# A two-layer encoder at 512 tokens: the feed-forward norm's factor goes into the operand from the third up block on

## Chip, cores and metric

The kernel runs on one core of one Trainium2 chip. The metric is device time in microseconds (us) of one execution. Three runs of the kernel before took 1310.16, 1311.35 and 1311.37 us; the median is 1311.35 us. Engines are named as in the profile: PE is TensorE (matmuls), PEld its weight loads, DVE is VectorE, ACT is ScalarE, POOL is GpSimd, SP the engine that issues the DMAs.

## The reference

Two layers, each an attention mixer, a cross-attention over 256 memory tokens and a feed-forward network with a depthwise convolution over positions; D_MODEL is 1024, D_FF is 2816, all in fp32. Only the feed-forward part matters here:

```python
def rms_norm(x, g):
    y = x32 * lax.rsqrt(jnp.mean(x32 * x32, axis=-1, keepdims=True) + EPS)
    return (y * g).astype(x.dtype)

def conv_ffn(h, w_up, conv_w, conv_b, w_down):      # h = rms_norm(x, norm_ffn[l])
    u = h @ w_up
    up = jnp.pad(u, ((0, 0), (1, 1), (0, 0)))
    u = up[:, :-2] * conv_w[0] + up[:, 1:-1] * conv_w[1] + up[:, 2:] * conv_w[2] + conv_b
    gate, val = jnp.split(u, 2, axis=-1)
    return (jax.nn.silu(gate) * val) @ w_down
```

The norm has a gain g per feature and a factor rsqrt(...) per token. The factor is the same for all features of a token, so it may be multiplied into h before the product with w_up or into u behind it.

## The kernel before

**Layout.** Activations lie transposed: 1024 features as 8 chunks of 128 partitions, 512 tokens along the free axis. `xT` holds the residual stream in fp32. Products are taken in fp32r with both operands split into a high and a low part; `mm3` issues three matmuls for each chunk: weight high times operand high, weight high times operand low, weight low times operand high.

**The norm's operand.** While the previous stage closes, `Norm.operand` writes for each chunk the high part of g times x (`ffn.hi`, on ACT) and its low part (`ffn.lo`, on DVE). These are two SBUF tiles of 8 x 512 columns with the tag `xg`, of which the pool has two buffers, so there is no room for a second pair. The token's factor isn't in them: it needs the sum over all chunks. `Norm.stat` and `Norm.spread` make it later as `ffn.rep`, 128 x 512, the factor of each token repeated on every partition.

**The up blocks.** The 22 blocks of 128 features of gate and value come in the order `UPS` (0, 2, 1, 3, ...). For each, `up_project` multiplies the 8 chunks with the block's two weight tiles (side 0 gate, side 1 value): 24 matmuls of 512 columns into one PSUM bank a side. Side 0 goes to the tag `sc`, side 1 to `tr`, with two banks each; the first block alone uses `mm`. `up_first` runs the first two blocks, and between them `ffn.stat()` and `ffn.spread()`. Then `up(UPS[n])` runs for n = 2 to 21, and from n = 5 on a `down_halved` step of the down projection stands behind each.

**Behind the product.** `up_finish` multiplies both PSUM sums by `ffn.rep` on DVE, in place. ACT then writes the centre tap and the bias into an SBUF tile, DVE adds the other taps from PSUM (two instructions of 504 columns and two of 7 for a side), ACT applies Silu, DVE multiplies gate and value, and `halved` splits the result and its sums of quarters into high and low for the down product (ACT copies, DVE subtractions).

**Weights.** Each weight tile comes by DMA into one of 3 `raw` buffers; ACT copies it to a high part, POOL subtracts to get the low part, 128 x 1024 each, into 4 buffers `hi` and 4 `lo`. A buffer comes free when PE has finished the block that read it.

**What sets the order.** No instruction is issued where it is written. `Taped` records every operation with its reads and writes; `Tape.plan` simulates the five engines with a table of costs and chooses an order for each engine; `Tape.play` (line 395 of before) issues it. So nearly all instructions carry line 395 in the profile, and a change in one place lets the planner reorder what stands behind it.

Of the kernel before, what the change touches and what calls it, by code (L numbers as in the profile page):

```python
# [14 lines left out]
ALU = mybir.AluOpType  # L15
# [11 lines left out]
KC = D // P  # L27
# [4 lines left out]
NF = D_FF // P  # L32
N_HALVED = [16, 16]
UPS = [j + (0, 1, -1, 0)[j % 4] if j < max(N_HALVED) else j for j in range(NF)]
N_COLS = 384
BEHIND = 5
EPS = 1e-6
BIG = 3.0e38
# [12 lines left out]
G_MIX, G_MQ, G_MKV, G_FFN, CW, CB = 0, 8, 16, 24, 32, 32 + 6 * NF  # L51
# [438 lines left out]
def encoder_kernel(ctx: ExitStack, tc: tile.TileContext, t: dict, out: list):  # L490
    nc = tc.nc
    tape = Tape()
    PE, ACT, DVE, POOL, SP = (
        Taped(tape, e, calls) for e, calls in zip(ENGINES, (nc.tensor, nc.scalar, nc.vector, nc.gpsimd, nc.sync)))
# [13 lines left out]
    def nm(s):  # L508
        uid[0] += 1
        return f"{s}_{uid[0]}"  # L510
# [10 lines left out]
    def rpair():  # L521

        hl = rtile((2, S))
        return hl[:, 0, :], hl[:, 1, :]

    def tmp(shape=(S,)):
        return tpool.tile([P, *shape], F32, tag="t", name=nm("t"))
# [10 lines left out]
    f = lambda ap: ap.bitcast(F32)  # L538
# [62 lines left out]
    def get_w(key, ahead=AHEAD):  # L601
        n = done[0]
        assert plan[n][0] == key, (plan[n][0], key)
        ahead = n + 1 + ahead
        while ahead < min(len(plan), n + 1 + AHEAD_HELD) and plan[ahead][4][1:] == "r":
            ahead += 1
        while len(ready) < min(len(plan), ahead):
            while len(raws) < min(len(plan), len(ready) + N_RAW):
                emit_raw()
            emit_split()  # L610
        while len(raws) < min(len(plan), len(ready) + N_RAW):
            emit_raw()
        done[0] += 1
        w = ready[n]
        ready[n] = None
        return w
# [32 lines left out]
    xT = [x[:, 0:S] for x in xg0]  # L649
    par = cpool.tile([P, DEPTH, NPAR], F32, name="par")  # L650
# [217 lines left out]
    for n in FIRST:  # L868
        if isinstance(n, (int, slice)):
            c, cs = (n, slice(0, S)) if isinstance(n, int) else (0, n)  # L870
            hi, lo, g = nn.hi[:, c, cs], nn.lo[:, c, cs], xg0[c][:, S : S + 1]
# [20 lines left out]
    for l in range(DEPTH):  # L892
# [599 lines left out]
        ffn = nn  # L1492
        acts = {}

        def up_project(j, side):
            pm = ps_t() if side else ps_s()
            gemm_T(pm, get_w(("up", j, side)), ffn.ops, range(KC), 0, KC - 1)
            return pm

        def up_first():  # L1500


            ws, us = [], []
            for side in range(2):
                ws.append(get_w(("up", 0, side)))
                us.append(ps_mm())
                gemm_T(us[side], ws[side], ffn.ops, range(KC - 1), 0, KC - 1)
            for side in range(2):
                gemm_T(us[side], ws[side], ffn.ops, [KC - 1], 0, KC - 1)
                if side == 0:  # L1510
                    ffn.stat()
            us1 = [up_project(UPS[1], 0)]
            ffn.spread()
            up_finish(0, us)
            us1.append(up_project(UPS[1], 1))
            up_finish(UPS[1], us1)

        def up(j):
            up_finish(j, [up_project(j, side) for side in range(2)])

        def up_finish(j, us):
            for side in range(2):
                DVE.tensor_mul(us[side], us[side], ffn.rep)
            cs = []
            for side in range(2):
                ch = side * NF + j
                u = us[side]
                w = [par[:, l, CW + i * 2 * NF + ch : CW + i * 2 * NF + ch + 1] for i in range(3)]
                cc = tmp()
                ACT.activation(cc, u, AF.Identity, bias=par[:, l, CB + ch : CB + ch + 1], scale=w[1])  # L1530
                for wi, dst, src in (
                    (w[0], slice(8, S), slice(0, S - 8)),
                    (w[0], slice(1, 8), slice(S - 8, S - 1)),
                    (w[2], slice(0, S - 8), slice(8, S)),
                    (w[2], slice(S - 8, S - 1), slice(1, 8)),
                ):
                    DVE.scalar_tensor_tensor(cc[:, dst], u[:, src], wi, cc[:, dst], op0=ALU.mult, op1=ALU.add)
                cs.append(cc)
            ACT.activation(cs[0], cs[0], AF.Silu)
            DVE.tensor_mul(cs[0], cs[0], cs[1])  # L1540
            if j < N_HALVED[l]:
                halved(j, cs[0])
                return
            acts[j] = rpair()
            ACT.copy(acts[j][0], cs[0])
            DVE.tensor_sub(acts[j][1], cs[0], f(acts[j][0]))
# [4 lines left out]
        def halved(j, u):  # L1551


            n = UPS.index(j)
            if n % 4 == 0:
                shared[:] = [rtile((2, 2, H))]
            if n % 2 == 0:
                waiting[n + 1] = u
                hl = shared[0][:, n // 2 % 2]
                ACT.copy(hl[:, 0], u[:, :H])  # L1560
                DVE.tensor_sub(hl[:, 1], u[:, :H], f(hl[:, 0]))
                return
            a, b = waiting.pop(n), u.rearrange("p (n q) -> p n q", n=2)
            hl, bh = shared[0][:, n // 2 % 2], rtile((2, 2, H))
            first, second = tmp((2, H)), tmp((2, H))
            hi, lo = rtile((4, H)), rtile((4, H))
            DVE.tensor_sub(first[:, 0], a[:, H:], a[:, :H])
            DVE.tensor_sub(second[:, 0], first[:, 0], b[:, 1])
            DVE.tensor_sub(first[:, 1], b[:, 1], a[:, H:])
            DVE.tensor_add(second[:, 1], b[:, 0], second[:, 0])  # L1570
            ACT.copy(bh[:, 0], b)
            DVE.tensor_sub(bh[:, 1], b, f(bh[:, 0]))
            for v, c in ((first, slice(0, 2)), (second, slice(2, 4))):
                ACT.copy(hi[:, c], v)
                DVE.tensor_sub(lo[:, c], v, f(hi[:, c]))
            q = {"11": (hl[:, 0], hl[:, 1]), "21": (bh[:, 0, 0], bh[:, 1, 0]), "22": (bh[:, 0, 1], bh[:, 1, 1])}
            for i, name in enumerate(("t1", "t3", "t2", "t4")):
                q[name] = hi[:, i], lo[:, i]
            quads[UPS[n - 1]] = q

        def down_halved(g, m):


            w = get_w(("down", g, m))

            def product(pm, a, b):
                for k in range(2):
                    mm3(pm, *w[a][k], *quads[4 * g + k][b], k == 0, k == 1)

            def pair(left, right):  # L1590
                pm = ps_mm()
                product(pm[:, :H], *left)
                product(pm[:, H:], *right)
                return pm

            left, right = (xT[m][:, c] for c in (slice(0, H), slice(H, S)))
            below = xT[m + 4].rearrange("p (n q) -> p n q", n=2)
            us = tmp((2, H))
            u, u2 = us[:, 0], us[:, 1]
            one = pair(("11", "11"), ("s2", "t2"))  # L1600
            ACT.copy(u, one[:, :H])
            DVE.tensor_add(left, left, one[:, :H])
            DVE.tensor_add(one[:, H:], one[:, H:], u)
            DVE.tensor_add(right, right, one[:, H:])
            ACT.copy(u2, one[:, H:])
            two = pair(("12", "21"), ("s4", "22"))
            DVE.tensor_add(xT[m], xT[m], two)
            three = pair(("22", "t4"), ("s1", "t1"))
            DVE.tensor_add(xT[m + 4], xT[m + 4], three)
            DVE.tensor_sub(right, right, three[:, H:])  # L1610
            four = ps_mm()[:, :H]
            product(four, "s3", "t3")
            DVE.tensor_add(four, four, u2)
            DVE.tensor_sub(below, below, four.unsqueeze(1).to_broadcast([P, 2, H]))
# [19 lines left out]
        def down_last(j0, nj):  # L1634
# [4 lines left out]
            SP.dma_start(gains, t["gfin"])  # L1639
            cs, tail = slice(0, N_COLS), slice(N_COLS, S)  # L1640
            ws = []
# [7 lines left out]
            for m in range(KC):  # L1649
                if m % 4 == 0:  # L1650
                    ws.extend(get_w(("down", n)) for n in range(len(ws), 3 + 3 * (m // 4)))
                rows.append(ps_mm()[:, :N_COLS])
                late = m < N_LATE
# [58 lines left out]
        for n in range(NF):  # L1712
            if n == 0:
                up_first()
            elif n > 1:
                up(UPS[n])
            if 0 <= n - BEHIND < N_HALVED[l]:
                down_halved(*divmod(n - BEHIND, 4))
# [159 lines left out]
```

## Time and profile before

| | |
|---|---|
| three runs, us | 1310.16, 1311.35, 1311.37 (median 1311.35) |
| the profiled execution, us | 1310.85 |
| its span, first to last instruction, us | 1308.8 |
| around the span, us | 2.05 |
| granted PE clock, share of full | 0.999 |
| DVE busy, us | 1058.4 (81%) |
| ACT busy, us | 739.2 (56%) |
| POOL busy, us | 808.9 (62%) |

The up blocks of layer 0 lie between about 300 and 600 us of the span, those of layer 1 between about 950 and 1270 us. In a row of the timeline the first number is the start in us, the second the time in which the row's instructions ran, then come engine, line, operation, output<-inputs (buffer numbers left out), shapes and count; in brackets stands how long the engine was idle ahead of it and what ended that. A PE row's time is that of the pipelined matmul up to its modelled end, so PE's pace is read from the starts.

### The profile page before, as it was taken

The numbers are of one execution on the slowest core, as the hardware profiler recorded it, in microseconds if no ns is written. First come the engines' busy times: TensorE is split into PE (matmuls) and PEld (weight loads), VectorE is DVE, ScalarE is ACT, GpSimd is POOL, SyncE is SP. The second block draws the span as 40 slices with busy tenths as digits, with TensorE's granted clock in tenths as the row PEclk, the third lists the DMA queues.
The fourth block names the chain that finished last, engine by engine and source line by source line (L and its number), as shares of the span: only waits on it lengthen the run. The fifth ranks groups of instructions, "written<-read, shape, count | busy, mean of one in ns | idle before, by whom it ended". The sixth has DMA issues, their size and how long they took to land.

```text
span 1308.8 us, 19578 instructions
## 1 busy us (share of the span) xinstructions
PE 1299.8 (99%) x6937; PEld 1121.7 (86%) x6937; DVE 1058.4 (81%) x2007; ACT 739.2 (56%) x1391; POOL 808.9 (62%) x607
## 2 busy tenths in 40 slices
PE   9999999999999999999999999999999999999997
PEld 8898888888888888888888988888888888888897
DVE  7679996766999998987555898956769999989865
ACT  7777686555545444544537767865645444444442
POOL 4465867627666677773726657774466667777651
PEclk9999999999999999999999999999999999999999
DMA  8752313313323333332355422232133333333321
GB/s 284 217 146 53 109 49 97 97 38 114 95 78 115 111 97 97 100 116 91 105 161 178 128 67 81 65 113 82 49 113 98 97 97 103 107 97 98 101 92 65
DMA packets 42609, 137.41 MB, mean 105 GB/s; under 512 B 5008, under 2 KB 8464, under 8 KB 42512
## 3 DMA queue, kind: packets, MB, share of 16 engines
q1 hardware_dynamic: 42080, 135.77, 34.4%
q8 instruction: 55, 0.90, 0.3%
q10 hardware_dynamic: 432, 0.39, 0.1%
q14 instruction: 42, 0.34, 0.1%
HBM read 126.18 MB, written 2.10 MB: 98 GB/s over the span
## 4 chain that ended last, share of the span: by engine, by line
PE 98%; DVE 1%; DMA 1%; ACT 0%; POOL 0%; issue 0%
PE mm L395 51%; PE sc L395 25%; PE tr L395 22%; DMA r<-r 1%; ACT t L395 0%; DVE t L395 0%; DVE s L395 0%; POOL t L395 0%; ACT r L395 0%; DVE sc L395 0%; DVE r L395 0%; ACT hi L395 0%; DVE xg L395 0%; ACT s L395 0%
## 5 line engine op out<-in xcount | busy, mean ns | idle before, releaser
L395 POOL TENSOR_TENSOR lo<-raw,hi 128x512 fp32r<-128x512 f32 (+2 forms) x236 | 438.3, 1870 | 305.0 <-ACT hi L395 304.4
L395 ACT CAST hi<-raw 128x512 fp32r<-128x512 f32 (+2 forms) x276 | 219.9, 817 | 185.7 <-PE sc L395 70.4
L395 PE MATMUL mm<-r,hi 128*128 128x512 f32 (+2 forms) x928 | 247.1, 346 | 0.0
L395 PE MATMUL sc<-xg,hi 128*128 128x512 f32 (+1 forms) x740 | 229.0, 391 | 0.0
L395 PE MATMUL tr<-xg,hi 128*128 128x512 f32 x672 | 207.1, 389 | 0.0
L395 PEld LDWEIGHTS mm<-r,hi 128*128 128x128 f32 x928 | 163.3, 189 | 21.6
L395 PE MATMUL mm<-r,lo 128*128 128x256 f32 (+2 forms) x496 | 165.6, 334 | 0.0
L395 PEld LDWEIGHTS sc<-xg,hi 128*128 128x128 f32 x740 | 137.1, 189 | 27.1 <-ACT hi L395 0.4
L395 PE MATMUL mm<-r,r 128*128 128x256 f32 (+2 forms) x1040 | 158.4, 293 | 0.0
L395 PEld LDWEIGHTS tr<-xg,hi 128*128 128x128 f32 x672 | 126.0, 188 | 26.1
L395 PEld LDWEIGHTS mm<-r,r 128*128 128x128 f32 x1040 | 142.4, 191 | 2.7
L395 POOL TENSOR_TENSOR r<-t,r 128x512 fp32r<-128x512 f32 x80 | 118.0, 1480 | 42.5 <-ACT r L395 42.2
L395 PE MATMUL sc<-xg,lo 128*128 128x512 f32 (+1 forms) x370 | 143.4, 389 | 0.0
L395 ACT CAST r<-t 128x512 fp32r<-128x512 f32 (+1 forms) x164 | 94.5, 588 | 86.4 <-DVE t L395 69.8
L395 PE MATMUL tr<-xg,lo 128*128 128x512 f32 x336 | 130.7, 389 | 0.0
L395 DVE TENSOR_TENSOR xT<-xT,mm 128x256 f32<-128x256 f32 (+2 forms) x216 | 116.6, 560 | 15.8 <-PE mm L395 9.5
L395 PE MATMUL mm<-xg,hi 128*128 128x512 f32 (+1 forms) x386 | 121.6, 394 | 0.0
L395 DVE TENSOR_TENSOR t<-t,t 128x512 f32<-128x512 f32 (+2 forms) x110 | 116.5, 1079 | 5.5 <-ACT t L395 2.9
L395 PE MATMUL mm<-hi,xg 128*128 128x512 f32 (+1 forms) x384 | 108.4, 358 | 0.0
L395 POOL TENSOR_SCALAR t<-t,s 128x512 f32<-128x512 f32 (+1 forms) x112 | 67.3, 616 | 65.2 <-DVE s L395 59.5
L395 PEld LDWEIGHTS mm<-r,lo 128*128 128x128 f32 x496 | 93.9, 189 | 9.5
L395 DVE TENSOR_TENSOR r<-t,r 128x512 fp32r<-128x512 f32 (+1 forms) x84 | 81.6, 992 | 8.3 <-ACT r L395 7.7
(138 smaller groups left out, 2422.9 us busy)
## 6 DMA issues: line engine op xcount, KB each, us to landing
raw<-in_w SPq DMA_DIRECT2D x207, 512.0 KB, 3.7
r<-r SPq DMA_DIRECT2D x30, 256.0 KB, 3.6
r<-in_bias SPq DMA_DIRECT2D x16, 384.0 KB, 4.6
raw<-in_w SPq DMA_DIRECT2D x8, 384.0 KB, 3.0
r<-in_memT SPq DMA_DIRECT2D x4, 512.0 KB, 7.1
xT<-in_w SPq DMA_DIRECT2D x7, 256.5 KB, 4.2
out<-xT SPq DMA_DIRECT2D x4, 384.0 KB, 3.4
r<-in_w SPq DMA_DIRECT2D x9, 128.0 KB, 4.1
```

Of the source, the lines that this page charges most:

```text
L395: call(*args, **kwargs)
```

## The change

From the third up block of each layer on (n = 2), the factor is in the operand. `scale_operands` is recorded once a layer, ahead of `up(UPS[2])`. For each of the 8 chunks it makes v = x * g * rep on DVE in a temporary (one instruction with two SBUF tensors), copies v to the high part on ACT and writes v minus the high part to the low part on POOL. High and low are the same tiles as before, overwritten in place: a chunk can be rewritten only when the second block's last matmul has read it. `up_finish` then leaves out its two multiplications by `ffn.rep` for the remaining 20 blocks. The first two blocks keep theirs.

```diff
-N_COLS = 384
+N_COLS, N_SCALED = 384, 2
...
+        scaled = []
+
+        def scale_operands():
+
+            scaled.append(True)
+            for c in range(KC):
+                v = tmp()
+                g = par[:, l, G_FFN + c : G_FFN + c + 1]
+                DVE.scalar_tensor_tensor(v, xT[c], g, ffn.rep, op0=ALU.mult, op1=ALU.mult)
+                hi, lo = ffn.ops[c]
+                ACT.copy(hi, v)
+                POOL.tensor_sub(lo, v, f(hi))
...
         def up_finish(j, us):
-            for side in range(2):
-                DVE.tensor_mul(us[side], us[side], ffn.rep)
+            if not scaled:
+                for side in range(2):
+                    DVE.tensor_mul(us[side], us[side], ffn.rep)
...
             elif n > 1:
+                if n == N_SCALED:
+                    scale_operands()
                 up(UPS[n])
```

How the planner then orders the engines is shown at the switch in layer 0; layer 1 has the same rows under other buffer numbers. Here `xg_637` is the operand's high part, `xg_638` its low part, `tr_772` the second block's side 1, and `xT_76` to `xT_79` are pairs of chunks of the residual.

On PE, before, from the end of the second block on; the third block's side 0 is `sc_783`, its side 1 (`tr_787`) follows when the 24 matmuls of side 0 are through:

```order
L395 MATMUL tr_772<-xg_638,hi_753 128x512
L395 MATMUL tr_772<-xg_637,lo_754 128x512
L395 MATMUL sc_783<-xg_637,hi_764 128x512
L395 MATMUL sc_783<-xg_638,hi_764 128x512
L395 MATMUL sc_783<-xg_637,lo_765 128x512
```

On PE, of the change, at the same place; the third block is now `sc_791` and `tr_795`:

```order
L395 MATMUL tr_772<-xg_638,hi_753 128x512
L395 MATMUL tr_772<-xg_637,lo_754 128x512
L395 MATMUL sc_791<-xg_637,hi_764 128x512
L395 MATMUL tr_795<-xg_637,hi_773 128x512
L395 MATMUL sc_791<-xg_638,hi_764 128x512
L395 MATMUL sc_791<-xg_637,lo_765 128x512
L395 MATMUL sc_791<-xg_637,hi_764 128x512
L395 MATMUL tr_795<-xg_638,hi_773 128x512
L395 MATMUL tr_795<-xg_637,lo_774 128x512
L395 MATMUL tr_795<-xg_637,hi_773 128x512
L395 MATMUL sc_791<-xg_638,hi_764 128x512
```

The two sides of the third block now run side by side: each chunk's six matmuls stand together, and the first that reads a chunk's low part is the third of its six. All other PE rows of the program are in the order of before; there are 5776 rows in both.

On DVE, of the change, behind the transposition that makes `rep_767`; before, the eight rows that write `t_783` to `t_790` weren't there, and `t_776`, the second block's side 0, went on at once:

```order
L395 TENSOR_TENSOR mm_756<-mm_756,rep_767 128x512
L395 SCALAR_TENSOR_TENSOR t_783<-xT_76,par,rep_767 128x512
L395 SCALAR_TENSOR_TENSOR t_784<-xT_76,par,rep_767 128x512
L395 SCALAR_TENSOR_TENSOR t_776<-sc_763,par,t_776 128x504
L395 SCALAR_TENSOR_TENSOR t_785<-xT_77,par,rep_767 128x512
L395 SCALAR_TENSOR_TENSOR t_786<-xT_77,par,rep_767 128x512
L395 SCALAR_TENSOR_TENSOR t_787<-xT_78,par,rep_767 128x512
L395 SCALAR_TENSOR_TENSOR t_788<-xT_78,par,rep_767 128x512
L395 SCALAR_TENSOR_TENSOR t_789<-xT_79,par,rep_767 128x512
L395 SCALAR_TENSOR_TENSOR t_790<-xT_79,par,rep_767 128x512
L395 SCALAR_TENSOR_TENSOR t_776<-sc_763,par,t_776 128x7
```

The taps of the first two blocks stand behind the eight products now, one row of them excepted. DVE has 1906 rows before and 1842 in the change: 80 multiplications less, 16 products more.

On POOL, of the change; before, the row on `lo_793` (then `lo_785`) was followed at once by the next weight's low part:

```order
L395 TENSOR_TENSOR lo_793<-raw_755,hi_792 128x1024
L395 TENSOR_TENSOR xg_638<-t_783,xg_637 128x512
L395 TENSOR_TENSOR xg_638<-t_784,xg_637 128x512
L395 TENSOR_TENSOR xg_638<-t_785,xg_637 128x512
L395 TENSOR_TENSOR xg_638<-t_786,xg_637 128x512
L395 TENSOR_TENSOR xg_638<-t_787,xg_637 128x512
L395 TENSOR_TENSOR xg_638<-t_788,xg_637 128x512
L395 TENSOR_TENSOR xg_638<-t_789,xg_637 128x512
L395 TENSOR_TENSOR xg_638<-t_790,xg_637 128x512
L395 TENSOR_TENSOR lo_797<-raw_766,hi_796 128x1024
```

All eight subtractions stand in one run, and `lo_797`, a weight of the fourth block, waits behind them. On ACT the copies of the first two chunks stand behind the first block's two centre taps, then the weight copy `hi_796`, whose buffer comes free with the last matmul of `tr_772`, then the copies of the other six chunks. SP's order of DMAs is unchanged.

## The prediction

> **What bounds the kernel now.** First the page: the span, the busy times, and the chain of work that ended last:
>
> ```profile
> span 1308.8 us, 19578 instructions
> ...
> PE 1299.8 (99%) x6937; PEld 1121.7 (86%) x6937; DVE 1058.4 (81%) x2007; ACT 739.2 (56%) x1391; POOL 808.9 (62%) x607
> ...
> PE 98%; DVE 1%; DMA 1%; ACT 0%; POOL 0%; issue 0%
> ```
>
> PE is busy for all but 9 us of the span and holds 98% of the chain. A busy PE may still run below its pace, so next I read its timeline where the third, fourth and fifth up block of layer 0 begin:
>
> ```profile
> 321.53 0.62 PE L395 MATMUL sc<-xg,hi 128*128 128x512 f32 x2
> 321.98 0.39 PE L395 MATMUL sc<-xg,lo 128*128 128x512 f32 x1
> 322.21 0.62 PE L395 MATMUL sc<-xg,hi 128*128 128x512 f32 x2
> ...
> 332.41 0.62 PE L395 MATMUL sc<-xg,hi 128*128 128x512 f32 x2
> ...
> 343.29 0.62 PE L395 MATMUL sc<-xg,hi 128*128 128x512 f32 x2
> ```
>
> Three matmuls take 322.21 - 321.53 = 0.68 us, 0.227 each. A block of 48 takes 332.41 - 321.53 = 10.88 us, which is 48 x 0.227, and so does the next. In these blocks PE waits for nothing, not for a tenth of a microsecond. Whatever DVE saves there, PE cannot give back; the change can only add a wait.
>
> **What is removed.** The multiplications by `rep`; the view of that tile's users counts them:
>
> ```profile
> L395 DVE TENSOR_TENSOR sc<-sc,rep x44: 683/689/700, 30.0 to 1260.9; 128x512 f32<-128x512 f32 x44
> L395 DVE TENSOR_TENSOR tr<-tr,rep x42: 686/690/700, 321.7 to 1266.3; 128x512 f32<-128x512 f32 x42
> ```
>
> 80 of these 86 go (2 sides, 20 blocks, 2 layers), at a median of 0.69 us: 55 of DVE's 1058 us. They lie beside matmuls that run without a gap, so for the path I take 0. The other end would be PE's 9 idle us of the whole span, but the blocks above hold none of them.
>
> **What is added, in the order of time.** Per layer: eight products on DVE, eight copies on ACT, eight subtractions on POOL, and on PE a wait for each chunk's low part. DVE of before around the switch in layer 0:
>
> ```profile
> 316.18 0.72 DVE L395 STREAM_TRANSPOSE rep<-tr 128x512 f32<-128x512 f32 x1 [5.70 <-PE tr L395]
> 316.93 0.70 DVE L395 TENSOR_TENSOR sc<-sc,rep 128x512 f32<-128x512 f32 x1
> 317.54 1.29 DVE L395 TENSOR_TENSOR mm<-mm,rep 128x512 f32<-128x512 f32 x2
> 318.73 1.77 DVE L395 SCALAR_TENSOR_TENSOR t<-sc,par,t 128x504 f32<-128x504 f32 x4
> ```
>
> POOL and ACT at the same time, and the row of `rep` in layer 1:
>
> ```profile
> 317.07 2.41 POOL L395 TENSOR_TENSOR lo<-raw,hi 128x1024 fp32r<-128x1024 f32 x1 [0.43 <-ACT hi L395]
> ```
>
> ```profile
> 315.94 1.05 ACT L395 CAST hi<-raw 128x1024 fp32r<-128x1024 f32 x1 [4.45 <-PE sc L395]
> 317.66 0.78 ACT L395 ACTIVATE t<-sc,par 128x512 f32<-128x512 f32 x1 [0.67 <-DVE sc L395]
> 318.34 1.44 ACT L395 ACTIVATE t<-mm,par 128x512 f32<-128x512 f32 x2
> 321.54 1.05 ACT L395 CAST hi<-raw 128x1024 fp32r<-128x1024 f32 x1 [1.76 <-issue]
> ...
> 329.13 0.61 ACT L395 CAST r<-t 128x512 fp32r<-128x512 f32 x1
> ```
>
> ```profile
> 962.19 0.72 DVE L395 STREAM_TRANSPOSE rep<-tr 128x512 f32<-128x512 f32 x1 [5.69 <-PE tr L395]
> ```
>
> The orders are the same until 318.73; there the first product is issued. PE wants the first low part at 321.98 (third matmul) and, with the two sides side by side, a further one every 6 x 0.227 = 1.36 us, the eighth at 331.50. So all hangs on how fast the low parts come. The old readers don't hold them up: the second block's side 1 begins 24 x 0.227 = 5.44 us ahead of 321.53 and lets go of a chunk every 0.68 us.
>
> A subtraction alone is short enough, but POOL and DVE hinder each other. DVE and POOL near the start of the program:
>
> ```profile
> 22.20 0.68 DVE L395 TENSOR_TENSOR lo<-raw,hi 128x512 fp32r<-128x512 f32 x1
> 22.80 1.77 DVE L395 TENSOR_TENSOR lo<-raw,hi 128x512 fp32r<-128x512 f32 x1
> ```
>
> ```profile
> 22.20 1.82 POOL L395 TENSOR_TENSOR lo<-raw,hi 128x512 fp32r<-128x512 f32 x1 [0.23 <-ACT hi L395]
> ...
> 22.20 3.53 POOL L395 TENSOR_TENSOR lo<-raw,hi 128x512 fp32r<-128x512 f32 x2 [0.23 <-ACT hi L395]
> 25.70 1.29 POOL L395 TENSOR_TENSOR t<-t,t 128x512 f32<-128x512 f32 x1
> ```
>
> POOL and DVE later, and DVE with POOL idle:
>
> ```profile
> 126.43 5.44 POOL L395 TENSOR_TENSOR lo<-raw,hi 128x512 fp32r<-128x512 f32 x4 [10.53 <-ACT hi L395]
> ```
>
> ```profile
> 126.89 2.57 DVE L395 SCALAR_TENSOR_TENSOR r<-r,par,r 128x256 fp32r<-128x256 f32 x2
> ```
>
> ```profile
> 11.30 1.41 DVE L395 SCALAR_TENSOR_TENSOR xg<-xT,xg 128x512 fp32r<-128x512 f32 x2
> ```
>
> Alone, POOL's operation takes 1.29 us (25.70). At 22.20 both engines begin one on two SBUF tensors: DVE ends at 22.88, POOL at 24.02, DVE's second at 24.57, POOL's second at 25.73. They go by turns, 1.16 for POOL and 0.55 for DVE, 1.71 a pair. The row at 126.89 has the products' own form, two SBUF tensors and a scalar: two of only 256 columns took 2.57 us beside POOL, where two of 512 took 1.41 with POOL idle (11.30). So I expect products and subtractions to take turns.
>
> [...]
>
> The walk: POOL holds the port until 317.07 + 2.41 = 319.48; the first product ends 0.55 later, at 320.03, the second at about 320.65. ACT has ended its centre taps by 319.78 and copies the first chunk by 320.70. Then DVE has one row on PSUM, and POOL runs the first subtraction alone, from 320.78 to 322.07. From there each of the six remaining products goes ahead of one subtraction: the seventh ends at 322.07 + 6 x 1.71 = 332.33. The copies (0.61 each) keep up, though the weight copy at 321.54 holds ACT until 322.59. With 0.08 for a handover (ACT's copy of 315.94 ends at 316.99, POOL starts at 317.07) PE begins on the seventh low part at 332.41 and 1.36 later, at 333.77, on the eighth, which it would have read at 331.50. **The wait is 2.27 us a layer.** In general it is 6 x (p - 1.36) + 0.17 for p us a pair. Bounds of p: 1.36, PE's own pace, if nothing hinders POOL (its 1.29 is then shorter), 0.17 us a layer; and 1.29 + 0.71 = 2.0 if both take their full time one behind the other, 4.0 us. I take the measured pair, 1.71.
>
> **What is late next.** The taps of the first two blocks stand behind the products, so PSUM banks come free later. The eighth product ends at 331.2. The rest of `sc_763` takes about 1.0 (of the 1.77 at 318.73), so its bank is free at 332.2; PE wants it at 332.41 + 2.27 = 334.7. ACT then has a copy, a table load, a Silu and a centre tap to run ahead of DVE's taps on `tr_772`:
>
> ```profile
> 323.29 1.28 ACT L395 ACT_TABLE_LOAD   x1
> 324.58 0.63 ACT L395 ACTIVATE t<-t 128x512 f32<-128x512 f32 x1
> ```
>
> 331.2 + 0.61 + 1.28 + 0.63 + 0.78 = 334.5; those taps end near 337.0, and PE wants the bank at 340.1. Going on like this I find the third block's side 0 free at about 344.2 (wanted at 345.6) and its side 1 at 349.7 (wanted at 351.0), with DVE meeting two of POOL's 2.4 us weight subtractions on the way. The margins are thin but positive: I count 0. At the other end two more such meetings, 4.8 us, against a margin of 1.4 would cost 3.4 us a layer; below 0 there is no room, as PE has no wait to lose. From then on each block spares DVE two multiplications, 1.4 us. The weight that now stands behind the subtractions, `lo_797`, ends near 333.6 + 2.4 = 336.0 and is wanted at 340.1.
>
> Layer 1 repeats layer 0 with 646.0 us added (962.19 against 316.18), so the sum is 2 x 2.27 = 4.5 us on the profiled execution's 1310.85: 1315.4 us. The median of the three runs lies 0.5 above that execution; beside it I forecast **1315.9 us**.
>
> **The rivals.** (1) **Not slower: the switch hides.** If the products got ahead of POOL, or POOL gave way less than at 22.20, interleaved PE, at 1.36 a chunk, would cover it: 2 x 0.17 = 0.3 us, 1311.7. It decides at p = 1.55, where the wait is 1.3 us a layer, 2.6 together: 0.2%, about what a measurement of this kernel can tell from no change. For it speaks only that POOL alone is faster than PE; against it, the rows with both engines at work. 16%. (2) **The backlog reaches PE**: banks come back late, 1.0 to 3.4 us a layer on top, 1317.9 to 1322.7. For it: the thin margins; against it: DVE's load falls with each block. 8%. (3) **The clock falls.** In this row of the windows PE idles for 0.77 of 10 us, and the granted clock is the column with 1.00:
>
> ```profile
> 0.00:10.00 10.00, 9.23 (x44) 8.18 (x45) 5.65 (x18) 7.08 (x17) 1.71 (x8) 1.00 0.71 218
> ```
>
> At the switch PE would idle for 2.3 of 13.1 us, in pieces of 0.35. If one such block ran at half clock its 10.88 us would double: up to 22 us for both layers, 1338. 4%. The Trainium skill, "TensorE: Matmul & The Clock Gate", section A second HAM failure mode, has micro-idles between groups of matmuls make the clock oscillate; the row doesn't bear it out, but its gaps are fewer. (4) **Faster by over 0.2%**: 2.6 of PE's 9 idle us would have to go, and its order outside the switch is unchanged. 2%.
>
> **How the numbers follow.** The forecast, 2.6 to 8 us slower, gets 70%; its own range is 1314.0 (p = 1.55) to 1319.4 (p = 2.0). The range is 1312.2 to 1320.5: it takes in a part of rival 1 below and a part of rival 2 above, and leaves out the rest. Faster 0.02; same 0.16 (rival 1); slower 0.82 (the forecast, rivals 2 and 3).
>
> **What would show it.** In the profile after: eight subtractions `xg<-t,xg` on POOL, near 1.7 us from one to the next; products `t<-xT,par,rep` on DVE stretched to about 1.7 us; the third block of either layer lasting 13.1 us instead of 10.88, the next ones 10.88 again, the clock at 1.00. I am wrong if the third block keeps 10.9 us (rival 1), if the blocks behind it are longer too (rival 2), or if the multiplications saved shorten anything on PE.

## The result, and the profile after

| | before | change |
|---|---|---|
| median of 8 runs each, us | 1311.09 (1309.96 to 1312.81) | 1315.46 (1314.29 to 1316.65) |
| ratio of times, 95% interval | | 1.0033 [1.0024, 1.0042] |
| span of the profiled execution, us | 1308.8 | 1312.9 |
| third up block, layer 0 / layer 1, us | 10.88 / 10.88 | 13.26 / 13.26 |
| DVE busy, us | 1058.4 | 1024.4 |

The change makes the kernel 4.4 us slower. First the page of the change:

```profile
span 1312.9 us, 19588 instructions
...
PE 1303.3 (99%) x6937; PEld 1120.2 (85%) x6937; DVE 1024.4 (78%) x1943; ACT 747.1 (57%) x1407; POOL 831.7 (63%) x623
...
PE 97%; POOL 1%; issue 0%; DMA 0%; ACT 0%; SPq 0%; DVE 0%
```

PE still reads 99% busy and has 3.5 us more of busy time, with as many matmuls as before. So the loss can't be found as idle time of PE. The starts of PE's rows show it. This is PE's timeline in the change, from the first matmul of the third block in layer 0 to the first of the fifth, with the same block of layer 1 behind it:

```profile
320.81 0.39 PE L395 MATMUL sc<-xg,hi 128*128 128x512 f32 x1
321.03 0.39 PE L395 MATMUL tr<-xg,hi 128*128 128x512 f32 x1
321.45 0.50 PE L395 MATMUL sc<-xg,hi 128*128 128x512 f32 x1
321.79 0.40 PE L395 MATMUL sc<-xg,lo 128*128 128x512 f32 x1
322.03 0.40 PE L395 MATMUL sc<-xg,hi 128*128 128x512 f32 x1
...
323.14 0.50 PE L395 MATMUL sc<-xg,hi 128*128 128x512 f32 x1
...
334.07 0.39 PE L395 MATMUL sc<-xg,hi 128*128 128x512 f32 x1
...
344.95 0.61 PE L395 MATMUL sc<-xg,hi 128*128 128x512 f32 x2
...
969.21 0.39 PE L395 MATMUL sc<-xg,hi 128*128 128x512 f32 x1
...
982.47 0.61 PE L395 MATMUL sc<-xg,hi 128*128 128x512 f32 x2
```

The third block takes 334.07 - 320.81 = 13.26 us, 2.38 more than before; the fourth takes 344.95 - 334.07 = 10.88 again; layer 1's third takes 13.26 too. Between the switches nothing changed: 969.21 - 334.07 = 635.14 us, against 967.54 - 332.41 = 635.13 in the kernel before. The third matmul of a chunk, the first that reads the low part, starts 0.42 us behind its forerunner (321.03 to 321.45) instead of 0.227, and the one behind it another 0.34 later. From chunk to chunk PE now needs 323.14 - 321.45 = 1.69 us, further on 1.71, not 1.36.

What it waits for is in the list of waits, on the row of the weight loads. The columns are engine, tile and line, then the releaser, the total in us, how often, and the longest:

```profile
PEld sc L395 <- POOL xg L395: 6.6, 14, 0.5
```

Fourteen times in the program (seven a layer) a weight load stands until POOL has written a low part. The wait is booked on PEld, while the matmul ahead is still counted as busy on PE. POOL and DVE at the switch in layer 0:

```profile
316.35 2.41 POOL L395 TENSOR_TENSOR lo<-raw,hi 128x1024 fp32r<-128x1024 f32 x1 [0.43 <-ACT hi L395]
320.09 12.77 POOL L395 TENSOR_TENSOR xg<-t,xg 128x512 fp32r<-128x512 f32 x8 [1.34 <-ACT xg L395]
```

```profile
315.46 0.72 DVE L395 STREAM_TRANSPOSE rep<-tr 128x512 f32<-128x512 f32 x1 [5.69 <-PE tr L395]
...
318.01 1.96 DVE L395 SCALAR_TENSOR_TENSOR t<-xT,par,rep 128x512 f32<-128x512 f32 x2
...
320.54 9.91 DVE L395 SCALAR_TENSOR_TENSOR t<-xT,par,rep 128x512 f32<-128x512 f32 x6
...
342.23 1.78 DVE L395 SCALAR_TENSOR_TENSOR t<-sc,par,t 128x504 f32<-128x504 f32 x4
```

Eight subtractions run without a break from 320.09 to 332.86; the first seven end 1.70 to 1.71 us apart. The seventh ends at 331.62, and PE's matmul that reads it starts at 331.67. Six products take 9.91 us beside them, 1.65 each. The users of `rep` over the whole program, with the least, median and greatest length in ns, say the same, and count what went:

```profile
L395 DVE SCALAR_TENSOR_TENSOR t<-xT,par,rep x16: 740/1776/1787, 318.0 to 977.1; 128x512 f32<-128x512 f32 x16
...
L395 DVE TENSOR_TENSOR sc<-sc,rep x4: 698/700/700, 30.3 to 964.6; 128x512 f32<-128x512 f32 x4
...
L395 DVE TENSOR_TENSOR tr<-tr,rep x2: 686/688/690, 331.4 to 979.8; 128x512 f32<-128x512 f32 x2
```

A product takes 0.74 us when nothing hinders it and 1.78 beside a subtraction. DVE lost 80 multiplications, 55 us, and its busy time fell by only 34, since the sixteen products are stretched by their turns with POOL and other rows moved as well. The windows of the third block show the clock, in the column behind the five engines' busy times:

```profile
320.80:334.10 13.30, 13.02 (x50) 8.49 (x49) 12.56 (x12) 7.28 (x11) 13.30 (x9) 1.00 0.06 23
```

The clock stays at 1.00; POOL is busy for the whole stretch. The span's +4.1 us is 2 x 2.38 = 4.76 for the switches, less 0.72 by which this execution was already ahead at the transposition that makes `rep` (315.46 against 316.18): a difference that arises before the change has any effect.

### The profile page after: what moved, and what is told of

It reads as the page before. It is cut to its first block, busy times and chain, and to the rows that moved or that the text cites. A ratio compares the mean times of both kernels' runs of the same rounds, so it can differ in the third digit from the quotient of the medians.

```text
span 1312.9 us, 19588 instructions
## 1 busy us (share of the span) xinstructions
PE 1303.3 (99%) x6937; PEld 1120.2 (85%) x6937; DVE 1024.4 (78%) x1943; ACT 747.1 (57%) x1407; POOL 831.7 (63%) x623
## 4 chain that ended last, share of the span: by engine, by line
PE 97%; POOL 1%; issue 0%; DMA 0%; ACT 0%; SPq 0%; DVE 0%
PE mm L395 52%; PE sc L395 24%; PE tr L395 21%; POOL xg L395 1%; DMA xT<-in_w 0%; SPq L395 0%; ACT xg L395 0%; DVE r L395 0%; ACT t L395 0%; POOL t L395 0%; ACT s L395 0%; ACT hi L395 0%; DVE s L395 0%
## 5 line engine op out<-in xcount | busy, mean ns | idle before, releaser
L395 POOL TENSOR_TENSOR lo<-raw,hi 128x512 fp32r<-128x512 f32 (+2 forms) x236 | 434.8, 1856 | 301.9 <-ACT hi L395 301.3
L395 ACT CAST hi<-raw 128x512 fp32r<-128x512 f32 (+2 forms) x276 | 220.1, 817 | 241.5 <-PE sc L395 90.1
L395 PE MATMUL mm<-r,hi 128*128 128x512 f32 (+2 forms) x928 | 247.1, 346 | 0.0
L395 PE MATMUL sc<-xg,hi 128*128 128x512 f32 (+1 forms) x740 | 232.9, 392 | 1.1 <-ACT xg L395 0.3
L395 PE MATMUL tr<-xg,hi 128*128 128x512 f32 x672 | 209.8, 389 | 0.0
L395 PEld LDWEIGHTS mm<-r,hi 128*128 128x128 f32 x928 | 163.2, 189 | 21.7
L395 PEld LDWEIGHTS sc<-xg,hi 128*128 128x128 f32 x740 | 136.8, 188 | 34.0 <-POOL xg L395 6.6
L395 PE MATMUL mm<-r,lo 128*128 128x256 f32 (+2 forms) x496 | 165.6, 334 | 0.0
L395 PE MATMUL mm<-r,r 128*128 128x256 f32 (+2 forms) x1040 | 158.4, 293 | 0.0
L395 PEld LDWEIGHTS tr<-xg,hi 128*128 128x128 f32 x672 | 126.0, 188 | 26.4
L395 PEld LDWEIGHTS mm<-r,r 128*128 128x128 f32 x1040 | 142.4, 191 | 2.7
L395 PE MATMUL sc<-xg,lo 128*128 128x512 f32 (+1 forms) x370 | 143.4, 388 | 0.0
L395 POOL TENSOR_TENSOR r<-t,r 128x512 fp32r<-128x512 f32 x80 | 116.3, 1458 | 35.6 <-ACT r L395 19.6
L395 DVE TENSOR_TENSOR xT<-xT,mm 128x512 f32<-128x512 f32 (+2 forms) x216 | 117.3, 560 | 19.6 <-PE mm L395 13.5
L395 PE MATMUL tr<-xg,lo 128*128 128x512 f32 x336 | 130.8, 389 | 0.0
L395 ACT CAST r<-t 128x512 fp32r<-128x512 f32 (+1 forms) x164 | 92.8, 587 | 54.9 <-DVE t L395 28.5
L395 PE MATMUL mm<-xg,hi 128*128 128x512 f32 (+1 forms) x386 | 121.5, 393 | 0.0
L395 DVE TENSOR_TENSOR r<-t,r 128x512 fp32r<-128x512 f32 (+1 forms) x84 | 99.0, 1202 | 27.1 <-ACT r L395 26.8
L395 PE MATMUL mm<-hi,xg 128*128 128x512 f32 (+1 forms) x384 | 108.4, 358 | 0.0
L395 DVE TENSOR_TENSOR t<-t,t 128x512 f32<-128x512 f32 (+2 forms) x110 | 101.5, 942 | 8.5 <-ACT t L395 4.9
L395 POOL TENSOR_SCALAR t<-t,s 128x512 f32<-128x512 f32 (+1 forms) x112 | 67.3, 617 | 63.4 <-DVE s L395 56.6
L395 PEld LDWEIGHTS mm<-r,lo 128*128 128x128 f32 x496 | 93.9, 189 | 9.5
```

What stands on the lines that cost most here:

```text
L395: call(*args, **kwargs)
```

## The experiments

The theory after the result: **DVE's products and POOL's subtractions take turns at SBUF**; a pair takes 1.71 us, and PE at 1.36 a chunk waits for the low parts. The rivals: the wait is made by something else in the chain (the copy on ACT, the new order of the sides on PE) and would stand without the turns; the multiplications removed bring a gain that the sum of 4.4 hides; a backlog on DVE has a part in it. Each edit below is made to the kernel with the change. With each edit the planner chooses its orders anew: only e8 keeps PE's order of the change row for row, and e3 has that of the kernel before. In e1, e2, e5 and e6 some matmuls of the next block stand among those of the block of the switch. A length below is therefore PE's time for 48 matmuls from the block's first one on, in layer 0 and in us; behind it stand the times beside the kernel before on the same chip:

| | third | fourth | fifth | time, us | before, us | ratio, 95% interval |
|---|---|---|---|---|---|---|
| before | 10.88 | 10.88 | 10.88 | | | |
| change | 13.26 | 10.88 | 10.88 | 1315.46 | 1311.09 | 1.0033 [1.0024, 1.0042] |
| e1: factor read from PSUM | 11.13 | 10.88 | 10.88 | 1310.66 | 1310.52 | 1.0002 [0.9993, 1.0011] |
| e2: switch two blocks later | 10.88 | 10.88 | 12.67 | 1319.07 | 1310.52 | 1.0065 [1.0053, 1.0078] |
| e3: removal alone | 10.88 | 10.88 | 10.88 | 1310.42 | 1310.52 | 1.0000 [0.9992, 1.0009] |
| e4: addition alone | 13.29 | 10.88 | 13.94 | 1321.39 | 1310.52 | 1.0083 [1.0069, 1.0097] |
| e5: every other product from PSUM | 12.34 | 11.35 | 10.88 | 1314.30 | 1310.34 | 1.0029 [1.0018, 1.0041] |
| e6: each product twice | 19.74 | 12.42 | 11.0 | 1332.57 | 1310.34 | 1.0169 [1.0155, 1.0182] |
| e7: subtraction on DVE | 12.61 | 13.11 | 11.0 | 1319.85 | 1310.34 | 1.0072 [1.0058, 1.0085] |
| e8: addition alone, planner blind to it | 13.26 | 13.52 | 11.71 | 1322.46 | 1310.34 | 1.0091 [1.0077, 1.0105] |

### e1: the products read the factor from PSUM

```diff
             scaled.append(True)
+            rep = ps_mm()
+            ACT.copy(rep, ffn.rep)
             for c in range(KC):
...
-                DVE.scalar_tensor_tensor(v, xT[c], g, ffn.rep, op0=ALU.mult, op1=ALU.mult)
+                DVE.scalar_tensor_tensor(v, rep, g, xT[c], op0=ALU.mult, op1=ALU.mult)
```

The products keep their number and their size; one of their two operands lies in PSUM, and the two change places in the instruction. The planner also moves taps between them.

> The factor is copied once a layer by ACT into a PSUM bank that is free then (tag mm), and the eight products read it from there, so each has one SBUF tensor and one PSUM tensor; number of products, copies, subtractions and PE's interleaving are those of the change. Theory (products and subtractions take turns because both engines work on two SBUF tensors): the subtractions follow each other in 1.25 to 1.3 us instead of 1.71, PE's third block lasts 10.9 to 11.3 us instead of 13.26, and the time is 1311.3 to 1312.0 us. Rival A (the chain product, copy, subtraction and its handovers is what is slow, wherever the operands lie): the block stays at 13 us and the time near 1315.5. Rival B (the late release of PSUM banks costs the time): one bank more is taken, so no gain, 1315.5 or more.

Measured: 1310.66 us, 0.14 above the kernel before, and a third block of 11.13 us. The group of the sixteen products (busy time, then ns of one, then idle time ahead), and POOL's timeline at the switch:

```profile
L395 DVE SCALAR_TENSOR_TENSOR t<-mm,par,xT 128x512 f32<-128x512 f32 x16 | 11.7, 741 | 0.0
```

```profile
321.47 2.55 POOL L395 TENSOR_TENSOR xg<-t,xg 128x512 fp32r<-128x512 f32 x2 [0.90 <-ACT xg L395]
324.30 5.07 POOL L395 TENSOR_TENSOR xg<-t,xg 128x512 fp32r<-128x512 f32 x4 [0.28 <-ACT xg L395]
329.32 2.41 POOL L395 TENSOR_TENSOR lo<-raw,hi 128x1024 fp32r<-128x1024 f32 x1
331.69 3.00 POOL L395 TENSOR_TENSOR xg<-t,xg 128x512 fp32r<-128x512 f32 x2
```

All sixteen products take 0.74 us, and four subtractions in a row 5.07, 1.27 each. So the turns go with the second SBUF operand, as the theory has it.

The time doesn't follow from that alone, since the planner gave this kernel another order as well. It put a weight subtraction ahead of the last two low parts, and the eighth comes at 334.69, 12.06 us behind the block's first matmul (322.63). In the change it comes 12.05 us behind (332.86 against 320.81), no later. PE doesn't wait for it here, because ten matmuls of the fourth block's side 0 stand ahead of the third block's last, which is the second of these rows:

```profile
335.57 0.39 PE L395 MATMUL tr<-xg,hi 128*128 128x512 f32 x1
335.80 0.39 PE L395 MATMUL tr<-xg,lo 128*128 128x512 f32 x1
```

In the change's order PE would want the eighth low part 331.50 - 321.53 = 9.97 us behind its first matmul, and would have waited some 2.1 us for this one. Without the weight subtraction, and with the products in time, two more steps of 1.27 behind the sixth low part (329.37) would bring the eighth 9.3 us behind, soon enough. Both are estimates from these rows: no run has the factor in PSUM together with the change's order. What e1 shows is the pace without turns, and that the copies on ACT and the rewriting in place, in this order, cost 0.25 us a layer at most. That turns at this pace make the wait is shown by the rows of the change, and by e5.

The version is only equal to the kernel before, a little better than expected: DVE is busy for 36.6 us less than there (1021.8), and PE, which sets the pace, has no work less.

### e3: the removal alone

```diff
             scaled.append(True)
-            for c in range(KC):
-                v = tmp()
...
-                POOL.tensor_sub(lo, v, f(hi))
```

> The multiplications behind the sums are left out from the third block on, and nothing is put in their place, so the factor is missing in 20 of 22 up blocks. Theory (PE is at its pace in the up blocks, so what DVE saves is worth nothing): DVE's busy time falls by 55 us, PE's blocks stay at 10.88 us and the time stays within 0.5 us of before, 1310.6 to 1311.6. Rival D (sparing DVE shortens something, and the change's 4.3 us are a larger cost less a gain): faster than before by 1 us or more, below 1310.

Measured: 1310.42 against 1310.52 us; every block 10.88. Its page:

```profile
PE 1299.0 (99%) x6937; PEld 1121.7 (86%) x6937; DVE 1005.4 (77%) x1927; ACT 736.4 (56%) x1391; POOL 805.1 (62%) x607
```

53 us of DVE are gone and the time has not moved. There is no gain hidden in the change's sum; its 4.4 us are all loss.

### e5: every other product from PSUM

```diff
+            rep = ps_mm()
+            ACT.copy(rep, ffn.rep)
...
-                DVE.scalar_tensor_tensor(v, xT[c], g, ffn.rep, op0=ALU.mult, op1=ALU.mult)
+                DVE.scalar_tensor_tensor(v, rep if c % 2 else ffn.rep, g, xT[c], op0=ALU.mult, op1=ALU.mult)
```

> As the run with the factor in PSUM, but only the products of chunks 1, 3, 5 and 7 read it there; those of 0, 2, 4 and 6 read the SBUF copy, as in the change. Theory (turns): half the turns are gone, so the mean pace of the subtractions is about 1.5 us and the third block lasts 11.2 to 12.2 us, between the 11.2 of all in PSUM and the 13.26 of none; the time is 1311.0 to 1313.5 us. Rival E (what helped was only that the planner ordered DVE otherwise once the rows were on PSUM): no value between the two is called for; the block is at one of the two ends.

Measured: 1314.30 us, above what was expected, with a third block of 12.34. Its subtractions end at 321.13, 322.84, 324.08, 325.78, 327.03 and 328.73: paces of 1.71, 1.24, 1.70, 1.25, 1.70, in step with where the product's operand lies. So the turns are taken product by product. The products from SBUF have their operands in e1's order too, so it isn't the swap that ended the turns there. The excess over the expectation is in POOL's rows behind them:

```profile
319.84 8.90 POOL L395 TENSOR_TENSOR xg<-t,xg 128x512 fp32r<-128x512 f32 x6 [1.33 <-ACT xg L395]
329.38 1.29 POOL L395 TENSOR_TENSOR xg<-t,xg 128x512 fp32r<-128x512 f32 x1 [0.65 <-ACT xg L395]
330.63 2.39 POOL L395 TENSOR_TENSOR lo<-raw,hi 128x1024 fp32r<-128x1024 f32 x1
332.99 1.74 POOL L395 TENSOR_TENSOR xg<-t,xg 128x512 fp32r<-128x512 f32 x1
```

The planner has put a weight subtraction of 2.39 us between the seventh and the eighth chunk; the eighth low part comes at 334.73. As in e1, matmuls of the fourth block fill a part of PE's time until then.

### e6: each product twice

```diff
                 DVE.scalar_tensor_tensor(v, xT[c], g, ffn.rep, op0=ALU.mult, op1=ALU.mult)
+                DVE.scalar_tensor_tensor(v, xT[c], g, ffn.rep, op0=ALU.mult, op1=ALU.mult)
```

> Each product is computed twice into the same tile, so DVE has two operations on two SBUF tensors for each subtraction of POOL; the output is that of the change. Theory (turns): a chunk takes 1.16 + 0.55 + 0.6, some 2.3 us, and the first low part comes a little later, so PE's third block lasts 16.5 to 18.0 us and the time is 1322 to 1326 us, more if the backlog reaches PE as well. Rival A (the chain product, copy, subtraction sets the pace, DVE's own load does not): the doubled product adds its 0.66 us once at the start only, the block lasts 13.5 to 14.5 us, 1316 to 1318.

Measured: 1332.57 us and a third block of 19.74, beyond every value expected. That it grew this far says that the products set the pace; that it grew by more than the theory's sum lies on POOL, as its rows and PE's show:

```profile
321.65 2.98 POOL L395 TENSOR_TENSOR xg<-t,xg 128x512 fp32r<-128x512 f32 x2 [2.66 <-ACT xg L395]
324.60 2.80 POOL L395 TENSOR_TENSOR lo<-raw,hi 128x1024 fp32r<-128x1024 f32 x1
```

```profile
328.65 0.79 PE L395 MATMUL sc<-xg,hi 128*128 128x512 f32 x1 [2.75 <-ACT xg L395]
...
330.61 0.63 PE L395 MATMUL sc<-xg,lo 128*128 128x512 f32 x1
331.04 0.63 PE L395 MATMUL sc<-xg,hi 128*128 128x512 f32 x1
331.46 0.63 PE L395 MATMUL tr<-xg,hi 128*128 128x512 f32 x1
```

A weight subtraction again stands between the chunks, holds DVE and so the next products, and PE idles for 2.75 us. From the first low part (322.93) to the eighth (341.06) 18.1 us pass; less the weight subtraction's 2.8 that is 2.2 us for each of the seven steps, near the theory's 2.3.

Behind the gap PE's matmuls start every 0.43 us instead of 0.227; the window of that stretch has the clock at half:

```profile
330.70:334.40 3.70, 3.70 (x10) 2.89 (x9) 3.70 (x5) 1.24 (x2) 1.76 (x2) 0.50 0.00 0
```

This slows PE but doesn't lengthen the block, since PE waits for operands again behind it:

```profile
338.48 0.50 PE L395 MATMUL sc<-xg,hi 128*128 128x512 f32 x1 [0.67 <-ACT xg L395]
```

Layer 1 bears it out: there the half clock lasts only from 986.7 to 990.0, in layer 0 from 327.9 to 334.6, and the block takes 19.73 us. As a measure of the pair's price e6 is rough, because of the weight subtraction.

### e7: the subtraction on DVE too

```diff
-                POOL.tensor_sub(lo, v, f(hi))
+                DVE.tensor_sub(lo, v, f(hi))
```

> The eight subtractions go to DVE, so DVE has product and subtraction of each chunk, 0.66 + 0.6 = 1.26 us when nobody disturbs it, and POOL only its weights. Theory (turns): each weight subtraction of POOL (2.4 us) that falls into the switch still stops DVE once, one or two of them; the third block lasts 11.5 to 13.5 us and the time is 1312 to 1316.5. Rival A (chain of three operations on engines that wait for each other): the chain is as long as before, 13.3 us or more, 1315.5 or more.

Measured: 1319.85 us, above the range, though the third block, 12.61, was within it. Here no subtraction of POOL's stands against the products, and DVE makes product and subtraction in 1.26 us together. But DVE meets POOL's weights, on DVE and POOL:

```profile
322.86 2.87 DVE L395 TENSOR_TENSOR xg<-t,xg 128x512 fp32r<-128x512 f32 x1
```

```profile
322.23 2.94 POOL L395 TENSOR_TENSOR lo<-raw,hi 128x1024 fp32r<-128x1024 f32 x1 [3.21 <-ACT hi L395]
```

One such meeting holds a subtraction of 0.69 us for 2.87. The products and subtractions now hold DVE for 10 us with hardly a tap between, and at 341.73 a DVE row of 256 columns meets another weight subtraction and takes 2.56 us instead of 0.43. So PE waits at the fifth block for its bank:

```profile
346.81 0.70 PE L395 MATMUL sc<-xg,hi 128*128 128x512 f32 x2 [1.86 <-DVE t L395]
```

That backlog, 2.2 us in the fourth block of either layer, is what the expectation left out. In layer 1 the fifth block takes 12.61 us too, against 11.0 in layer 0. There the granted clock was at half behind PE's wait:

```profile
997.50:1000.80 3.30, 3.30 (x10) 2.54 (x9) 3.27 (x5) 0.94 (x2) 2.60 (x2) 0.50 0.30 58
```

### e2: the switch two blocks later

```diff
-N_COLS, N_SCALED = 384, 2
+N_COLS, N_SCALED = 384, 4
```

> The switch is made ahead of the fifth block instead of the third (4 blocks keep their multiplications a layer, 18 are spared). The factor is ready two blocks earlier than it is needed, so most products can be made while the old operand is still being read. Theory (turns between products and subtractions): only products that are left when the first subtraction starts cost anything; the subtractions come every 1.3 to 1.5 us, PE's fifth block lasts 11.0 to 12.0 us in each layer and the time is 1311.5 to 1313.5 us. Rival A (chain of copy, subtraction and handover): 13 us for that block, 1315.5. Rival C (rewriting in place has to wait for the old readers): the wait would be the same or larger, 1315.5 or more.

Measured: 1319.07 us; expected was no more than 1313.5. The block of the switch, now the fifth, takes 12.67. The planner let the taps run between the products; that spread them, but one product still took 2.94 us, and the last two 1.77 and 1.78. The larger loss is behind, where the down projection begins:

```profile
372.85 0.74 PE L395 MATMUL mm<-r,r 128*128 128x256 f32 x4 [1.45 <-DVE r L395]
```

The products delay the block's tail on DVE, and with one block between the switch and the first down product, PE waits 1.45 us in each layer for its operand. Switch and backlog come to 2 x (1.8 + 1.45) = 6.5 of the 8.6 us. Of the other 2, some 1.65 are lost ahead of the switch: the third block of layer 0 begins at 323.18, in the kernel before at 321.53. PE waits there in an earlier stage, where the planner has set another order too:

```profile
145.72 0.72 PE L395 MATMUL mm<-r,hi 128*128 128x512 f32 x2 [1.18 <-DVE xT L395]
```

So e2 doesn't measure the switch alone.

### e4 and e8: the addition alone

```diff
         def up_finish(j, us):
-            if not scaled:
-                for side in range(2):
-                    DVE.tensor_mul(us[side], us[side], ffn.rep)
+            for side in range(2):
+                DVE.tensor_mul(us[side], us[side], ffn.rep)
```

> The operand is scaled as in the change and the 80 multiplications behind the sums stay too, so 20 of 22 up blocks have the factor twice. Theory: the wait at the switch is the whole cost, 2.4 us a layer, so the time is that of the change, 1315.0 to 1316.2; DVE's load falls by nothing behind the switch, so this also asks how thin the margins are. Rival B (the backlog on DVE reaches PE): blocks behind the third last longer than 10.88 us and the time is 1317 or more. Rival D (the saving on DVE pays back a part): 1317 or more too, but with the third block longer or PE gaps elsewhere.

Measured for e4: 1321.39 us, above the theory's 1315.0 to 1316.2. The third block was as in the change, 13.29; the fifth took 13.94. PE there:

```profile
351.65 0.86 PE L395 MATMUL mm<-r,hi 128*128 128x256 f32 x5 [0.74 <-ACT hi L395]
353.53 0.39 PE L395 MATMUL mm<-r,hi 128*128 128x256 f32 x1 [1.03 <-DVE r L395]
```

The planner had moved six matmuls of the first down product between the two sides of the fifth block, where their operands weren't ready. So e4 doesn't tell whether the multiplications themselves are to blame. e8 keeps them too, but the planner takes them to cost nothing, and PE's order is the change's, row for row:

```diff
+            if self.name == "tensor_tensor" and tag_of(self.reads[-1].tensor) == "rep":
+                return 1.0, 1.0
...
         def up_finish(j, us):
-            if not scaled:
-                for side in range(2):
+            for side in range(2):
+                if scaled:
+                    DVE.tensor_tensor(us[side], us[side], ffn.rep, op=ALU.mult)
+                else:
                     DVE.tensor_mul(us[side], us[side], ffn.rep)
```

> As the run that keeps the 80 multiplications beside the scaling (20 of 22 up blocks have the factor twice), but the planner counts those multiplications at next to nothing, so that PE's order is that of the change, row for row. Theory: the 2.9 us a layer that the other run had behind the switch came from six matmuls of the down product that the planner had put ahead of their operands; with PE in the change's order the third block lasts 13.26 us, the rest keep 10.88, and the time is 1315.0 to 1316.5 us. Rival B (DVE's backlog needs the spared multiplications to be worked off, or it reaches PE): PE waits again behind the switch, at sums or at operands of the first down products, and the time is 1317 or more.

Measured for e8: 1322.46 us. The theory's 1315.0 to 1316.5 fell; rival B, the backlog, holds. PE and DVE at the end of the fourth block (L397 is this kernel's L395):

```profile
345.08 0.39 PE L397 MATMUL tr<-xg,lo 128*128 128x512 f32 x1
347.95 0.70 PE L397 MATMUL sc<-xg,hi 128*128 128x512 f32 x2 [2.48 <-DVE t L397]
```

```profile
342.55 0.69 DVE L397 TENSOR_TENSOR sc<-sc,rep 128x512 f32<-128x512 f32 x1
343.15 2.96 DVE L397 TENSOR_TENSOR t<-t,t 128x256 f32<-128x256 f32 x2
346.03 1.78 DVE L397 SCALAR_TENSOR_TENSOR t<-sc,par,t 128x504 f32<-128x504 f32 x4
```

The third block's multiplication stands in DVE's row, two instructions behind it meet a weight subtraction and take 2.96 us, and the taps that free the bank end at 347.81 where PE could have begun at 345.31. In the change these taps begin at 342.23 and end at 344.01. The fourth block loses 2.6 us and the fifth 0.8 to 0.9 in either layer: 7 us that the spared multiplications keep off PE.

## Why the prediction was right

The forecast was 1315.9 us, the measured median is 1315.46; the change was foretold as slower, and is. By its steps:

- **PE runs at its pace, so nothing saved on DVE can come back.** Right. The removal alone (e3) saved 53 us of DVE and 0 of the time; e1, with neither turns nor multiplications, is equal to the kernel before, in an order of its own.
- **Products and subtractions take turns, 1.71 us a pair.** Right in kind and size. Beside subtractions a product takes 1.78 us instead of 0.74, PE's chunks come 1.69 to 1.71 us apart, and e1 and e5 show that it is the second SBUF operand which makes the turn.
- **The wait is 2.27 us a layer.** It is 2.38. The walk was right in place: the seventh low part was forecast for 332.33 on the time of before and came at 331.62, which is 332.34 when the 0.72 by which this execution was ahead is added. The 0.11 it lacked is PE's restart: behind a matmul that waited for a low part the next follows 0.34 us later instead of 0.227 (321.45 to 321.79), and the prediction let PE go on at pace at once.
- **Sum and time.** 2 x 2.38 = 4.76 us against 4.5 forecast; the medians differ by 4.37. The forecast's 0.4 above the measured median is within the scatter of the runs. That the medians' difference lies nearer to 4.5 than the trace's 4.76 does is scatter too, and no merit of the walk.
- **What is late next: 0.** Right, and as thin as said. The third block's side 0 was free at 344.01 and wanted at 344.95: 0.94 us to spare, where the prediction had 1.4. Its side 1 had more room than foretold: free at 346.44 and wanted at 350.39, 3.95 us instead of 1.3. e8 shows how little would have used it up.
- **The removal is worth 0.** Right, with an addition: that holds for the removal alone. Beside the new work on DVE the spared multiplications are what kept the backlog, rival 2, from PE (e8: 1322.46). The prediction named that the load falls by 1.4 us a block, and gave it no price.
- **The rivals.** That the switch hides (1) would have needed a pair under 1.55 us; only with an operand in PSUM does that come about. The backlog (2) didn't reach PE in the change, but did in e2, e7 and e8. The clock (3) stayed at 1.00 in the change. The prediction's row of 0.00:10.00 couldn't speak against this rival: its column reads 1.00, although matmuls of 256 columns start every 0.21 us there from 4.82 to 5.46 and every 0.12 from 5.76 on. In the change the starts themselves say it, 0.23 us apart between the waits. The Trainium skill, "GPSIMD Engine Reference", section Specifications, counts Vector instructions with two SBUF inputs among those that contend with GpSimd. The trace agrees: 1.78 us for a product beside a subtraction, 0.74 without.

## What to carry to other kernels

Where PE runs without a gap, as here, work taken off another engine is worth nothing by itself (e3), and work put in front of PE costs its full excess over PE's pace: 6 chunks x (1.71 - 1.36) = 2.1 of the 2.38 us a layer. Before giving one step of a chain to DVE and the next to POOL, look at where their operands lie. With two SBUF operands on both, the engines took turns; with one of DVE's in PSUM, its instruction took 0.74 us beside the same subtractions (e1). When an edit lets a planner choose again, compare PE's order before the time is put down to the edit. And look for the wait at the weight loads and at the distance of the starts, as PE's busy share doesn't show it.

## What the runs showed of the hardware that was not expected

- The clock can fall behind one longer gap, but the gap's length alone doesn't tell when. In e6 PE idles from 325.90 to 328.65; the granted clock was 1.00 from 325.9 to 327.8 and 0.50 from 327.9 to 334.6, so it fell some 2.0 us into the gap. In e7 a gap of 1.85 us in layer 1 was followed by 0.50, and one of 1.86 in layer 0 was not; nor were e8's gaps of 2.48 and 2.45 us. In the change, seven waits of up to 0.5 us in 13.3 us left it at 1.00. The Trainium skill, "TensorE: Matmul & The Clock Gate", section What's actually happening, has the clock halved behind an idle window of about 3.4 us; here less recorded idle time than that was enough. The same page's section A second HAM failure mode: psum-queue depth-cycling, with micro-idles between groups of matmuls, is not borne out by the change's waits.
- A matmul behind one whose operand came late follows at 0.34 us, not 0.227. Its own weight load begins late as well, 0.11 us behind the other's (321.55 and 321.44). Over the seven waits of a layer only the last such loss counts, as the others end in the next wait: 0.34 - 0.23 = 0.11 us.
- A POOL instruction holds a DVE instruction with two SBUF operands for all its length: 2.87 us for one of 0.69 beside a weight subtraction of 1024 columns, which ends at 325.17, the DVE instruction 0.56 later (e7).
